# High and low parts of two weight matrices made by casting and accumulating transfers instead of by two engines

## The chip, the cores and the metric

The kernel runs on one core of one Trainium2 chip. The metric is device time in microseconds (us) for one execution of the whole layer; a profile of one execution stands beside it. The engines are named as in the profile: PE does matrix products, ACT (ScalarE) and DVE (VectorE) do elementwise work from on-chip memory and from the product banks, POOL (GpSimd) does elementwise work in on-chip memory only, and SP issues transfers. All five run their own queue in order; semaphores tie them together.

## The reference

One decoder layer over 512 tokens of width 1024, in float32, in three residual steps:

```python
y = hybrid_mixer(rms_norm(x, pre_mix_g[l]), w_in[l], attn_gn_g[l], ret_gn_g[l], w_out[l])
x = x + rms_norm(y, post_mix_g[l])
y = memory_cross_attn(rms_norm(x, pre_mem_g[l]), mem, mem_norm_g[l],
                      w_q_mem[l], w_kv_mem[l], w_o_mem[l])
x = x + rms_norm(y, post_mem_g[l])
y = swiglu(rms_norm(x, pre_ffn_g[l]), w_gate_up[l], w_down[l])
x = x + rms_norm(y, post_ffn_g[l])
```

The mixer is an input projection, eight heads of dilated window attention beside four heads of chunked retention, and an output projection. The cross attention takes its keys and values from 256 memory rows: `mh = rms_norm(mem, mem_norm_g)`, then `k, v = split(mh @ w_kv, 2)`. The feed-forward step is `(silu(h @ w_gate) * (h @ w_up)) @ w_down` with a hidden width of 2816.

## The kernel before

Products are made in the reduced format fp32r, in which PE takes 512 columns in one pass. To keep float32 accuracy every operand is held as a pair: a high part, which is the value rounded to fp32r, and a low part, which is the value minus the high part. `mm3` (L82) makes one product of two pairs from three matrix products: high by high, high by low, low by high (L84, L85, L86).

Weights come in chunks of 128 partitions x 2048 columns, 1 MB each, in a fixed list (L96): 14 of w_in, 8 of w_kv, 4 of w_out, 4 of w_q, 4 of w_o, 22 of w_gu and 11 of w_dn. `load` (L101) takes the next chunk of the list: SP issues a transfer into one of two `raw` buffers, and then `split` (L88) makes the pair in two halves of 1024 columns. For each half, ACT copies the raw values into the high part with rounding (L90), and DVE subtracts the high part from the raw values into the low part (L91). `take` (L120) hands a chunk over and calls `load` for the chunks after it, two ahead unless told otherwise. The two parts of a pair lie in two units of a pool `up` of 20 units, which the other large tiles share: transposed activations, probabilities, residual rows, the hidden values `af`. A transfer into `raw` waits only for a free raw buffer; the copy into the high part waits for a free unit.

A scheduler places the instructions of each engine in one queue from the order of the program, the free units and its own costs; what an engine finds at the head of its queue it waits for. `order` below means those queues.

Around the change the work is this. The memory keys and values (`mem_keys`, `mem_values`) are cut into twelve units of work that are put between the units of the attention heads (`filler`). Keys use w_kv chunks 0 to 3, two units `kf` to a chunk, and POOL makes the low part `kTl` of each key unit (L539). Values use chunks 4 and 5 together, then 6 and 7 together, for two blocks of rows each, and POOL makes their low part `vml` (L551). The residual rows x are loaded a second time behind the last key units. In the memory block (`mem_block`) PE makes the output projection of the cross attention for one block of 128 tokens at a time; `residual` and `normed` follow with sums of squares on ACT (L624, L153), a reciprocal square root by three Newton steps on [128, 1] tiles (`rsqrt`, L137 to L141), and the wide products on DVE (L626, L630, L635). The small steps are done on the engine that is passed as `e`: POOL in all four memory blocks and in block 3 of the mixer. The result h is transposed on PE (tp) into `h3`, the input of the gate and up projections. Those run chunk by chunk: 24 products into g and 24 into u for each of 22 chunks, then silu on ACT (L817) and a product on DVE (L820). Chunks 0 and 1 are first done for 256 tokens only, while the norms of blocks 2 and 3 are finished.

Of the kernel before, what the change touches and what calls it, by code (L numbers as in the profile page):

```python
# [11 lines left out]
F32 = mybir.dt.float32  # L12
# [4 lines left out]
ALU = mybir.AluOpType  # L17
# [21 lines left out]
def hybrid_layer(ctx, tc, t, out):  # L39
    nc = tc.nc  # L40
# [9 lines left out]
    def uname(p):  # L50
        cnt[0] += 1
        return f"{p}{cnt[0]}"
# [4 lines left out]
    def unit(name, dt=F32):  # L57
        return up.tile([P, 2048], dt, tag="u", name=uname(name))

    def pair(name):  # L60
        return unit(name + "h", F32R), unit(name + "l", F32R)
# [4 lines left out]
    def row(name):  # L66
        return wk.tile([P, D], F32, tag="w4k", name=uname(name), bufs=2)

    def junk():
        return wk.tile([P, D], BF16, tag="junk", name=uname("junk"), bufs=1)  # L70

    def small(shape, name):
        big = math.prod(shape[1:]) > 8
        return sm.tile(shape, F32, tag="big" if big else "tiny", name=uname(name), bufs=2 if big else 32)
# [13 lines left out]
    def split(src, hi, lo, scale=None):  # L88
        if scale is None:
            nc.scalar.copy(hi, src)  # L90
            nc.vector.tensor_sub(lo, src, hi.bitcast(F32))  # L91
        else:
            nc.scalar.mul(hi, src, scale)
            nc.vector.scalar_tensor_tensor(lo, src, scale, hi.bitcast(F32), op0=ALU.mult, op1=ALU.subtract)

    chunks = [(name, i) for name, idx in (  # L96
        ("w_in", range(14)), ("w_kv", range(8)), ("w_out", (2, 3, 0, 1)), ("w_q", range(4)), ("w_o", range(4)),
        ("w_gu", range(FT)), ("w_dn", range(FT // 2))) for i in idx]
    loaded = {}

    def load(pieces=1, swap=False):  # L101
        key = chunks.pop(0)
        src = t[key[0]][key[1]]
        raw = rawp.tile([P, 2048], F32, tag="raw", name=uname("raw"))
        w = pair("w")
        n = 2048 // pieces
        for i in range(pieces):
            c = slice(i * n, (i + 1) * n)
            nc.sync.dma_start(raw[:, c], src[:, c])
        n = 2048 // max(2, pieces)  # L110
        for i in range(max(2, pieces)):
            c = slice(i * n, (i + 1) * n)
            if swap and i == 0:
                nc.vector.tensor_copy(w[0][:, c], raw[:, c])
                nc.vector.tensor_sub(w[1][:, c], raw[:, c], w[0][:, c].bitcast(F32))
            else:
                split(raw[:, c], w[0][:, c], w[1][:, c])
        loaded[key] = w
# [8 lines left out]
    def ahead(name, i):  # L127
        while (name, i) in chunks:
            load()
# [20 lines left out]
    def row_rstd(rows, n, width, name, eps=EPS, e=None):  # L150
        ss = small([P, n], name + "s")
        for i, r in enumerate(rows):
            nc.scalar.activation(junk()[:, :width], r, AF.Square, accum_out=ss[:, i:i + 1])  # L153
        v = small([P, n], name + "v")
        (e or nc.vector).tensor_scalar(v, ss, 1.0 / width, eps, op0=ALU.mult, op1=ALU.add)
        return rsqrt(v, n, name, e)

    def load_rows(name):
        x = [unit("x") for _ in range(2)]
        for i in range(2):  # L160
            nc.sync.dma_start(x[i].rearrange("p (b d) -> p b d", b=2),
                              t["x"][i * 256:(i + 1) * 256, :].rearrange("(b p) d -> p b d", p=P))
        return [x[b // 2][:, (b % 2) * D:(b % 2 + 1) * D] for b in range(TB)]
# [12 lines left out]
            nc.tensor.matmul(ps[:, b * P:(b + 1) * P], lhsT=ones, rhs=dg, start=True, stop=True)  # L176
        nc.vector.tensor_copy(dst, ps[:, :n * P])

# [1 line left out]
    gT = cp.tile([P, 3, KT], F32, name="gT")  # L180
    nc.scalar.dma_start(gT, t["gT"])
    hT = [pair("hT") for _ in range(2)]
# [24 lines left out]
    x = load_rows("x")  # L207
# [41 lines left out]

    w_rqk.clear()  # L250

# [1 line left out]
    def tok_proj(c0, name, evict):  # L253
        ws = []

        def one(b):
            if b == 0:
                ws[:] = [take("w_in", c0, 1), take("w_in", c0 + 1, 2)]
            ps = bank(name)
            for k in range(KT):  # L260
                mm3(ps, hx(k, b * P, P), part(ws[k // 4], (k % 4) * 512, 512), k == 0, k == KT - 1)
            if b == TB - 1:
                ws.clear()
            evict(b, ps)

        return [lambda b=b: one(b) for b in range(TB)]
# [33 lines left out]
            nc.tensor.transpose(ps[:, b * P:(b + 1) * P], src[:, c:c + P], ident)  # L300
        split(ps, *yx(k, 0, S), gT[:, 2, k:k + 1])

# [1 line left out]
    off = [0, 512, 1024, 896]  # L304
    inn, key, state = {}, {}, {}

# [58 lines left out]
    def ret_out(h):  # L365
        y_transposed(rg, 4 + h)

# [1 line left out]
    qk = [unit("qk", F32R) for _ in range(4)]  # L369
    kl = unit("kl", F32R)  # L370
    av = unit("av")
# [46 lines left out]
    def evict_av(b, ps):  # L418
        nc.scalar.mul(av[:, b * 512:(b + 1) * 512], ps, rstd0[:, b:b + 1])

# [1 line left out]
    scale = AD ** -0.5  # L422
    poff = [512 + 384, 1024, 512, 0]
    sbank = [(2, 0), (2, 256), (1, 0), (0, 0)]
# [46 lines left out]
    def att_values(h):  # L471
        pr, hh = h // 2, h % 2
        rows = slice(hh * 64, hh * 64 + 64)
        if hh == 0:
            oTb[pr] = bank("oT")
        u = pTs.pop(h)
        for kb in range(TB):
            nc.tensor.matmul(oTb[pr][rows, kb * P:S], lhsT=av[:, kb * 512 + h * AD:kb * 512 + (h + 1) * AD],
                             rhs=u[:, off[kb]:off[kb] + S - kb * P], start=kb == 0, stop=kb == TB - 1)
        if hh == 1:  # L480
            ot = work("ot")
            nc.scalar.copy(ot, oTb.pop(pr))
            oTb[pr] = ot
# [23 lines left out]
    def att_out(pr):  # L507
        y_transposed(ya, pr)

# [1 line left out]
    mem = {}  # L511

    def mem_prepare():
# [72 lines left out]
    for i in range(AH):  # L586
# [10 lines left out]
        if i % 3 == 2:  # L597
            filler()
        att_values(i)
# [1 line left out]
    x = load_rows("x")  # L601
    g1 = load_gain("post_mix_g")
    ret_out(0)
# [12 lines left out]
    def residual(pss, b, g, e=None, cuts=((0, 512), (512, 512))):  # L616
        e = e or nc.vector
        ss = small([P, len(cuts)], "ps")
        z = row("z")
        v = small([P, 1], "pv")  # L620
        for i, (c0, n) in enumerate(cuts):
            c = slice(c0, c0 + n)
            ps = pss[c0 // 512][:, c0 % 512:c0 % 512 + n]
            nc.scalar.activation(junk()[:, :n], ps, AF.Square, accum_out=ss[:, i:i + 1])  # L624
            e.tensor_scalar(v, ss[:, i:i + 1], 1.0 / D, v if i else EPS, op0=ALU.mult, op1=ALU.add)
            nc.vector.tensor_mul(z[:, c], ps, g[:, c])  # L626
        rs = rsqrt(v, 1, "pr", e)
        for c0, n in cuts:
            c = slice(c0, c0 + n)
            nc.vector.scalar_tensor_tensor(x[b][:, c], z[:, c], rs, x[b][:, c], op0=ALU.mult, op1=ALU.add)  # L630

    def normed(b, g, e=None):
        rs = row_rstd([x[b]], 1, D, "nr", e=e)
        h = row("h")
        nc.vector.scalar_tensor_tensor(h, x[b], rs, g, op0=ALU.mult, op1=ALU.mult)  # L635
        return h
# [12 lines left out]
    def out_proj(bs, lhs, ws, ks, name, outer, mid=None):  # L649
        pss = {b: [bank(name) for _ in range(2)] for b in bs}  # L650

        def one(b, n, i):
            k = ks[i]
            mm3(pss[b][n], lhs(k, b), part(ws[k // 2], (k % 2) * D + n * 512, 512), i == 0, i == KT - 1)

        for c in range(outer):
            for b in bs:
                for n in range(2):
                    for i in (2 * c, 2 * c + 1):
                        one(b, n, i)  # L660
        for b in bs:
            for n in range(2):
                if mid and (b, n) == (bs[-1], 1 if len(bs) == 1 else 0):
                    mid()
                for i in range(2 * outer, KT):
                    one(b, n, i)
        return pss
# [8 lines left out]
    def mix_half(hf, mid=None):  # L676
        bs = (2 * hf, 2 * hf + 1)
        pss = out_proj(bs, y_lhs, w_out, order, "o1", 2, mid)
        hs = []
        for b in bs:  # L680
            e = nc.gpsimd if b == 3 else nc.vector
            residual(pss[b], b, g1, e)
            hs.append(normed(b, g2, e))
        return hs
# [83 lines left out]
    wo = [take("w_o", c, 0) for c in range(4)]  # L768
    g3 = load_gain("post_mem_g")
# [6 lines left out]
    nat = tuple(range(KT))  # L776
    g4 = load_gain("pre_ffn_g")
    h3 = [pair("h3") for _ in range(2)]

    def mem_block(b, mid=None):  # L780
        residual(out_proj((b,), o_lhs, wo, nat, "o2", 0, mid)[b], b, g3, nc.gpsimd)
        return normed(b, g4, nc.gpsimd)

    def h3_block(h, b):
        transposed(h, lambda half: [a.rearrange("p (k s) -> p k s", k=4) for a in h3[half]], S, b * P)
# [15 lines left out]
    to_h3(ha, 1)  # L801
    hc = mem_block(3)

# [1 line left out]
    af = []  # L805

    def gx(k, c0, n):
# [15 lines left out]
    for f in range(2):  # L823
        w, pg, pu = take("w_gu", f), bank("g"), bank("u")
# [9 lines left out]
    for f in range(2, FT):  # L834
        w, pg, pu = take("w_gu", f), bank("g"), bank("u")
# [23 lines left out]
    for c in range(FT // 2 - NL):  # L859
        if c % 2 == 0:  # L860
            split_a(c // 2)
        w = take("w_dn", c)
# [111 lines left out]
```

## Time and profile before

| what | value |
|---|---|
| device time, median of 2 runs | 830.46 us (830.09 to 830.82) |
| span of the profiled execution, first to last instruction | 828.5 us |
| median less span | 1.96 us |
| PE busy | 807.9 us (98%) |
| DVE busy | 396.6 us (48%) |
| ACT busy | 305.4 us (37%) |
| POOL busy | 132.8 us (16%) |
| transfers | 85.86 MB, 104 GB/s over the span |
| mean granted TensorE clock | 0.991 |

The page gives no separate device time for the profiled execution. Its span is set beside the median of the runs, and the difference of 1.96 us is carried along as what lies around the span. A row that groups instructions gives their sum, their mean in ns and the idle time of the engine ahead of them. A product's row lasts longer than its slot, since products overlap in the array: the distance between two starts is what one costs.

### The profile page before, as it was taken

To read this page: it belongs to the slowest core of one execution; us is meant where nothing else is said; L and a number is where in the kernel's file an instruction comes from. 1 tells how busy PE (TensorE), PEld (TensorE's weight loads), DVE (VectorE), ACT (ScalarE), POOL (GpSimd) and SP (SyncE) were. 2 spreads that over 40 slices of the span, in tenths; PEclk is the share of its full clock that TensorE was granted. 3 is DMA by queue.
4 is the path that set the end of the run, shared out by engine and by line. 5 is a ranking of instruction groups with operands and counts; after the bars stand their busy time and mean duration, and the time that the engine had idled before them with its cause. 6 is when DMAs were issued, how large, how long until landed. Compare 5 with 4: busy or idle time off the path is not lost. (4 is left out here: it accounts for less than half of the span.)

```text
span 828.5 us, 10220 instructions
## 1 busy us (share of the span) xinstructions
PE 807.9 (98%) x4108; PEld 675.7 (82%) x4108; DVE 396.6 (48%) x766; ACT 305.4 (37%) x537; POOL 132.8 (16%) x176
## 2 busy tenths in 40 slices
PE   9979999999999999999999899999999999999996
PEld 7768888877777878999988788888888888888884
DVE  5595168764565657758446441405050314222144
ACT  5504333466464733445435232222130305332110
POOL 0161024410110100300036300000000004236000
PEclk9998999999999999999999999999999999999998
DMA  8726212221124440524002340505050322521011
GB/s 305 291 77 236 94 51 87 73 95 52 51 70 175 163 153 0 197 109 153 1 1 102 127 153 1 203 1 203 1 203 1 121 82 74 182 102 51 1 51 51
DMA packets 15519, 85.86 MB, mean 104 GB/s; under 512 B 1904, under 2 KB 1904, under 8 KB 6896
## 3 DMA queue, kind: packets, MB, share of 16 engines
q1 hardware_dynamic: 14752, 84.16, 27.7%
q10 hardware_dynamic: 720, 1.06, 0.3%
q8 instruction: 32, 0.52, 0.3%
q14 instruction: 15, 0.12, 0.0%
HBM read 83.11 MB, written 2.10 MB: 103 GB/s over the span
## 5 line engine op out<-in xcount | busy, mean ns | idle before, releaser
L91 DVE TENSOR_TENSOR wl<-raw,wh 128x1024 fp32r<-128x1024 f32 (+1 forms) x135 | 166.5, 1267 | 102.6 <-ACT wh L90 70.2
L90 ACT CAST wh<-raw 128x1024 fp32r<-128x1024 f32 (+1 forms) x135 | 133.8, 1042 | 95.3 <-DMA raw<-in_w_in 38.1
L820 DVE TENSOR_TENSOR af<-sg,u 128x512 f32<-128x512 f32 x22 | 15.1, 686 | 133.7 <-PE u L86 133.7
L846 POOL TENSOR_TENSOR al<-af,ah 128x512 fp32r<-128x512 f32 x22 | 34.6, 1605 | 257.5 <-ACT ah L845 243.3
L84 PE MATMUL g<-h3h,wh 128*128 128x512 f32 (+1 forms) x192 | 72.1, 375 | 0.0
L84 PE MATMUL u<-h3h,wh 128*128 128x512 f32 (+1 forms) x192 | 71.7, 373 | 0.0
L85 PE MATMUL g<-h3l,wh 128*128 128x512 f32 (+1 forms) x192 | 71.3, 371 | 0.0
L86 PE MATMUL g<-h3h,wl 128*128 128x512 f32 (+1 forms) x192 | 71.3, 371 | 0.0
L85 PE MATMUL u<-h3l,wh 128*128 128x512 f32 (+1 forms) x192 | 71.3, 371 | 0.0
L86 PE MATMUL u<-h3h,wl 128*128 128x512 f32 (+1 forms) x192 | 71.3, 371 | 0.0
L84 PE MATMUL dn<-wh,ah 128*128 128x512 f32 x176 | 68.5, 389 | 0.0
L85 PE MATMUL dn<-wl,ah 128*128 128x512 f32 x176 | 68.5, 389 | 0.0
L86 PE MATMUL dn<-wh,al 128*128 128x512 f32 x176 | 68.5, 389 | 0.0
L817 ACT ACTIVATE sg<-g 128x512 f32<-128x512 f32 x22 | 13.1, 598 | 149.2 <-PE g L86 123.0
L84 PEld LDWEIGHTS g<-h3h,wh 128*128 128x128 f32 x192 | 36.5, 190 | 6.5 <-ACT h3h L90 0.2
L84 PEld LDWEIGHTS u<-h3h,wh 128*128 128x128 f32 x192 | 36.6, 191 | 6.3
L85 PEld LDWEIGHTS g<-h3l,wh 128*128 128x128 f32 x192 | 36.2, 188 | 6.4
L86 PEld LDWEIGHTS g<-h3h,wl 128*128 128x128 f32 x192 | 36.2, 188 | 6.2
L85 PEld LDWEIGHTS u<-h3l,wh 128*128 128x128 f32 x192 | 36.2, 188 | 6.2
L86 PEld LDWEIGHTS u<-h3h,wl 128*128 128x128 f32 x192 | 36.1, 188 | 6.1
L84 PEld LDWEIGHTS dn<-wh,ah 128*128 128x128 f32 x176 | 33.0, 188 | 6.9
L86 PEld LDWEIGHTS dn<-wh,al 128*128 128x128 f32 x176 | 33.0, 188 | 6.9
(267 smaller groups left out, 1752.8 us busy)
## 6 DMA issues: line engine op xcount, KB each, us to landing
raw<-in_w_gu SPq DMA_DIRECT2D x22, 1024.0 KB, 4.8
raw<-in_w_in SPq DMA_DIRECT2D x12, 1024.0 KB, 5.1
raw<-in_w_dn SPq DMA_DIRECT2D x11, 1024.0 KB, 4.7
raw<-in_w_kv SPq DMA_DIRECT2D x8, 1024.0 KB, 4.7
x<-in_x SPq DMA_DIRECT2D x4, 1024.0 KB, 10.2
raw<-in_w_out SPq DMA_DIRECT2D x4, 1024.0 KB, 5.3
raw<-in_w_q SPq DMA_DIRECT2D x4, 1024.0 KB, 5.3
raw<-in_w_o SPq DMA_DIRECT2D x4, 1024.0 KB, 4.7
```

The lines of the kernel that those rows point to most:

```text
L84: nc.tensor.matmul(o, lhsT=sh, rhs=mh, start=start, stop=False)
L85: nc.tensor.matmul(o, lhsT=sh, rhs=ml, start=False, stop=False)
L86: nc.tensor.matmul(o, lhsT=sl, rhs=mh, start=False, stop=stop)
L90: nc.scalar.copy(hi, src)
L91: nc.vector.tensor_sub(lo, src, hi.bitcast(F32))
L817: nc.scalar.activation(sg, pg, AF.Silu)
L820: nc.vector.tensor_mul(af[-1][:, (f % 4) * S:(f % 4 + 1) * S], sg, pu)
L846: nc.gpsimd.tensor_sub(lo[:, c], af[i][:, c], hi[:, c].bitcast(F32))
```

## The change

In `load`, chunks of w_kv and w_gu go another way. POOL issues a transfer from the weight straight into the high part, with a cast to fp32r on the way. ACT then writes the negated high part over 2048 columns into the low part. POOL issues a second transfer of the same 1 MB that adds the weight onto it, so that the low part becomes weight minus high part. The other weights are loaded as before. Separately, the small steps of `residual` and `normed` that ran on POOL (four memory blocks, and block 3 of the mixer) go to DVE.

```diff
     def load(pieces=1, swap=False):
         key = chunks.pop(0)
         src = t[key[0]][key[1]]
+        if key[0] in ("w_kv", "w_gu"):
+            w = pair("w")
+            nc.gpsimd.dma_start(w[0], src)
+            nc.scalar.mul(w[1], w[0].bitcast(F32), -1.0)
+            nc.gpsimd.dma_start(w[1], src, accum_op=ALU.add)
+            loaded[key] = w
+            return
         raw = rawp.tile([P, 2048], F32, tag="raw", name=uname("raw"))
...
-            e = nc.gpsimd if b == 3 else nc.vector
+            e = nc.vector
             residual(pss[b], b, g1, e)
             hs.append(normed(b, g2, e))
...
-        residual(out_proj((b,), o_lhs, wo, nat, "o2", 0, mid)[b], b, g3, nc.gpsimd)
-        return normed(b, g4, nc.gpsimd)
+        residual(out_proj((b,), o_lhs, wo, nat, "o2", 0, mid)[b], b, g3, nc.vector)
+        return normed(b, g4, nc.vector)
```

The added lines move the later lines of the file by 7. Below, H(k) is the casting transfer of chunk k of w_kv, N(k) the negation on ACT, and L(k) the accumulating transfer.

POOL's queue before, from the third-last key unit to the end of the memory values (kTl is the low part of the keys, vml that of the values):

```order
L539 TENSOR_TENSOR kTl_1524<-kf_2014,kTh_1523 128x256
L539 TENSOR_TENSOR kTl_1524<-kf_2074,kTh_1523 128x256
L539 TENSOR_TENSOR kTl_1524<-kf_2126,kTh_1523 128x256
L551 TENSOR_TENSOR vml_1526<-vf_2220,vmh_1525 128x512
L551 TENSOR_TENSOR vml_1526<-vf_2304,vmh_1525 128x512
L551 TENSOR_TENSOR vml_1526<-vf_2386,vmh_1525 128x512
L551 TENSOR_TENSOR vml_1526<-vf_2415,vmh_1525 128x512
```

POOL's queue now, at the same place (wh_2029 and wl_2030 are chunk 4, 2164 and 2165 chunk 5, 2169 and 2170 chunk 6, 2324 and 2325 chunk 7):

```order
L546 TENSOR_TENSOR kTl_1518<-kf_2002,kTh_1517 128x256
L546 TENSOR_TENSOR kTl_1518<-kf_2059,kTh_1517 128x256
L108 DMA wl_2030<-in_w_kv 128x2048
L546 TENSOR_TENSOR kTl_1518<-kf_2111,kTh_1517 128x256
L106 DMA wh_2164<-in_w_kv 128x2048
L106 DMA wh_2169<-in_w_kv 128x2048
L108 DMA wl_2165<-in_w_kv 128x2048
L108 DMA wl_2170<-in_w_kv 128x2048
L558 TENSOR_TENSOR vml_1520<-vf_2199,vmh_1519 128x512
L558 TENSOR_TENSOR vml_1520<-vf_2283,vmh_1519 128x512
L106 DMA wh_2324<-in_w_kv 128x2048
L108 DMA wl_2325<-in_w_kv 128x2048
```

H(5) now stands behind the low part of the last key unit, and H(7) behind the low part of the second value block.

ACT's queue before, from the first to the last sum of squares of memory block 3 (raw_4188 and raw_4260 are gate/up chunks):

```order
L624 ACTIVATE junk_4133,ps_4130<-o_4080 128x512
L90 CAST wh_4189<-raw_4188 128x1024 x2
L90 CAST wh_4261<-raw_4260 128x1024 x2
L624 ACTIVATE junk_4137,ps_4130<-o_4081 128x512
L153 ACTIVATE junk_4155,nrs_4154<-x_2231 128x1024
```

ACT's queue now, at the same place (wl_4159 is gate/up chunk 2, wl_4228 chunk 3):

```order
L631 ACTIVATE junk_4109,ps_4106<-o_4056 128x512
L631 ACTIVATE junk_4113,ps_4106<-o_4057 128x512
L107 ACTIVATE wl_4159<-wh_4158 128x2048
L160 ACTIVATE junk_4131,nrs_4130<-x_2210 128x1024
L107 ACTIVATE wl_4228<-wh_4227 128x2048
```

The two sums of squares of the projection now follow each other, and one negation, which waits for the casting transfer of gate/up chunk 2, stands ahead of the sum of squares of the new x.

## Prediction

> **What bounds the kernel now.** First the page: the span and the shares of the engines. Then the waits of PE, since PE is busy nearly all the time.
>
> ```profile
> span 828.5 us, 10220 instructions
> PE 807.9 (98%) x4108; PEld 675.7 (82%) x4108; DVE 396.6 (48%) x766; ACT 305.4 (37%) x537; POOL 132.8 (16%) x176
> ...
> PE rv L85 <- DVE wl L91: 5.2, 1, 5.2
> PE tp L792 <- DVE h L635: 4.0, 1, 4.0
> PE warm L215 <- POOL ones L196: 1.0, 1, 1.0
> ```
>
> PE sets the time. In 828.5 us it waits twice for more than a microsecond once it has begun its work: 5.2 us for a low part of w_in, which the change doesn't touch, and 4.0 us for h of the last memory block. No wait is on a chunk of w_kv or w_gu. So whatever is taken off DVE and ACT there can win little, and the questions are whether the 4.0 us go, and whether the new way of loading is in time everywhere.
>
> The price list comes from the groups, from the windows (columns: window, length, busy time of PE, PEld, DVE, ACT and POOL, granted clock, share of the transfer engines, GB/s) and from the issues (median us to landing last).
>
> ```profile
> L91 DVE TENSOR_TENSOR wl<-raw,wh 128x1024 fp32r<-128x1024 f32 (+1 forms) x135 | 166.5, 1267 | 102.6 <-ACT wh L90 70.2
> L90 ACT CAST wh<-raw 128x1024 fp32r<-128x1024 f32 (+1 forms) x135 | 133.8, 1042 | 95.3 <-DMA raw<-in_w_in 38.1
> ...
> 268.00:272.00 4.00, 4.00 (x21) 3.31 (x20) 2.15 (x10) 0.22 (x1) 0.00 (x0) 1.00 1.02 421
> 490.00:710.00 220.00, 220.00 (x972) 182.22 (x971) 61.13 (x60) 54.44 (x67) 13.04 (x8) 1.00 0.27 96
> ...
> raw<-in_w_kv SPq DMA_DIRECT2D x8, 1024.0 KB, 4.7
> ...
> x<-in_x SPq DMA_DIRECT2D x2, 1024.0 KB, 8.6
> ```
>
> A product of 512 columns takes a slot of 220.00 / 972 = 0.226 us. With all engines busy 421 GB/s flow, so 1 MB costs 2.5 us of the transfer engines; a 1 MB load lands after 4.7 us, so 2.2 us lie around it. Two x loads issued together, 2 MB, land after 8.6 us.
>
> **What is removed, and where it lay.** Thirty chunks no longer use ACT's two copies and DVE's two subtractions: 60 x 1.267 = 76 us of DVE work go. ACT's 60 x 1.042 = 63 us come back as 30 negations over 2048 columns, 2.1 us each at two halves' price. PE waited for none of it, so the gain is nothing, and if the estimate of the negation is off, ACT's idle 63% covers it.
>
> **The small norm steps go to DVE.** Two late products of memory block 3, the chain behind it on POOL, and the same steps on DVE at the end of the kernel (start, length, engine, line):
>
> ```profile
> 447.96 0.39 PE L85 MATMUL o<-wl,oTxh 128*128 128x512 f32 x1
> ...
> 452.27 0.39 PE L86 MATMUL o<-wh,oTxl 128*128 128x512 f32 x1
> ...
> 454.73 2.26 POOL L625 TENSOR_SCALAR pv<-ps,pv 128x1 f32<-128x1 f32 x1 [0.61 <-ACT junk L624]
> ...
> 461.44 0.27 POOL L141 TENSOR_SCALAR pry<-prw,pry 128x1 f32<-128x1 f32 x1
> 464.51 0.19 POOL L155 TENSOR_SCALAR nrv<-nrs 128x1 f32<-128x1 f32 x1 [2.81 <-ACT junk L153]
> ...
> 467.42 0.26 POOL L141 TENSOR_SCALAR nry<-nrw,nry 128x1 f32<-128x1 f32 x1
> ...
> 821.48 0.21 DVE L625 TENSOR_SCALAR pv<-ps,pv 128x1 f32<-128x1 f32 x1 [4.69 <-ACT junk L624]
> 821.61 0.68 DVE L626 TENSOR_TENSOR z<-dn,g 128x512 f32<-128x512 f32 x1
> ...
> 824.13 1.42 DVE L630 SCALAR_TENSOR_TENSOR x<-z,pry,x 128x512 f32<-128x512 f32 x2
> ```
>
> The first half took 461.71 - 454.73 = 7.0 us on POOL and takes 824.13 - 821.48 = 2.65 on DVE; the second 467.68 - 464.51 = 3.2 against 2.65 - 0.68 = 2.0. That is 5.5 us earlier, more than the 4.0 that PE waits. The negation of gate/up chunk 2 stands ahead of the sum of squares of x in ACT's queue. Its casting transfer goes out when the product at 447.96 releases its unit; by the prices below it lands at 454 and is negated by 456, before x is ready near 457.6 (last product 452.3, its sum of squares some 1.2, then 2.65 and 1.42). So it costs nothing; it would if that transfer took over 7 us.
>
> ```profile
> 458.25 1.03 PE L792 MATMUL tp<-ident,h 128*128 128x128 f32 x8
> ...
> 469.06 1.97 PE L792 MATMUL tp<-ident,h 128*128 128x128 f32 x8 [4.02 <-DVE h L635]
> ...
> 62.09 0.79 PE L85 MATMUL rv<-wl,hTh 128*128 128x512 f32 x1 [5.16 <-DVE wl L91]
> ...
> 66.09 0.48 PE L85 MATMUL rv<-wl,hTh 128*128 128x512 f32 x1
> ...
> 64.00:66.00 2.00, 2.00 (x6) 1.61 (x5) 2.00 (x3) 0.00 (x0) 0.00 (x0) 0.50 0.43 74
> ```
>
> A long wait also costs clock. After the 5.16 us one the clock is at 0.50, and nine slots take 66.09 - 62.09 = 4.0 us instead of 2.0: 2.0 us lost. After the 4.02 us one eight transposes take 1.97 instead of 1.03; I count 1.2 us. **Gain: 4.0 + 1.2 = 5.2 us.**
>
> **The memory values, first wait.** Before, chunks of w_kv were fetched into raw buffers ahead of their unit. Now the high part's transfer needs the unit, the negation needs the transfer, the second transfer needs the negation, and POOL issues both between its own work, in order. H(5) stands behind the low part of key unit 7, so it goes out late.
>
> ```profile
> 253.78 0.72 POOL L539 TENSOR_TENSOR kTl<-kf,kTh 128x256 fp32r<-128x256 f32 x1 [5.64 <-ACT kTh L538]
> ...
> 252.00 0.28 PE L86 MATMUL mk<-memTh,wl 128*128 128x256 f32 x1
> 252.12 0.60 PE L490 MATMUL otr<-ident,ot 128*128 128x128 f32 x4
> ...
> 252.65 2.37 PE L478 MATMUL oT<-pT,av 128*64 128x512 f32 x8
> ...
> 256.01 0.48 PE L84 MATMUL mv<-wh,memTh 128*128 128x512 f32 x1
> ...
> 271.35 0.39 PE L86 MATMUL mv<-wh,memTl 128*128 128x512 f32 x1
> 271.58 1.03 PE L300 MATMUL yt<-ident,rg 128*128 128x128 f32 x8
> 272.45 1.47 PE L300 MATMUL yt<-ident,ya 128*128 128x128 f32 x12
> 273.68 0.47 PE L84 MATMUL mv<-wh,memTh 128*128 128x512 f32 x1
> ...
> 274.21 1.29 POOL L551 TENSOR_TENSOR vml<-vf,vmh 128x512 fp32r<-128x512 f32 x1 [7.21 <-ACT vmh L550]
> ```
>
> H(5) can be issued from 253.78 + 0.72 = 254.5 us. The two x loads now take the units of chunk 3, free at about 252.1 when the last key product is done, and L(4) goes out at that time too. An accumulating transfer must read its target as well as its source. No row shows one; its bounds are 2.5 us of the engines (any 1 MB) and 10 us (twice the 2 MB pair), and I take 5.0, since the pair of x loads, 8.6 us to landing, is the nearest row to 2 MB moved. A cast has no row either; I take 2.5. For POOL's issue I take 1 us, between 0.2 and 2.3, the ends of its small rows in the memory block. So the engines have 5.0 + 5.0 + 2.5 = 12.5 us of work from 252.1; H(5) lands at 264.6 + 1.1 = 265.7, N(5) ends at 267.8, L(5) lands 1 + 5.0 + 2.2 = 8.2 later, at 276.0. PE, which in the new order does 13 products, one head's oT and four transposes (20 take 273.68 - 271.58 = 2.1, so 0.42) before it needs L(5), is there at 256.0 + 2.9 + 2.4 + 0.4 = 261.7. **Wait: 14.3 us; 8.6 with every transfer at 2.5, 25 with 10 and the slow issue.**
>
> What the Trainium skill says of the price: in Collectives: The Full Stack, section "The bandwidth ceiling: the fold count and why AG ≠ RS ≠ AR", an add in the transfer engines is itself free but reads two sources, so it halves the rate (ratio 1.93). By that rule this wait is the 14.3, by a plain copy's price 8.6; no run here shows it yet.
>
> **Second wait.** H(7) stands behind the low part of value block 1: from that block's last product, 271.35, to the end of the row at 274.21 + 1.29 = 275.5, are 4.15 us. Then H(7) 1 + 4.7, N(7) 2.1, L(7) 8.2: 20.2 us in all. PE meanwhile has 2.3 (to 273.68) + 24 products 5.4 + 4 transposes 0.4 + 2 products 0.5 + 18 output products 4.1 = 12.7. **Wait: 7.5 us; 3.6 to 14.** N(7) also stands ahead of ACT's copies of the first w_out chunk, but PE needs those before it needs L(7), so they only divide the wait. Both waits are long enough to cost the clock: 2 x 2.0 = 4 us.
>
> **Gate and up.** A chunk is 48 x 0.226 = 10.9 us of PE, and H and L cost 2.5 + 5.0 = 7.5 us of the transfer engines, with the units free four to five chunks ahead and the negation some 2.5 chunks (27 us) ahead of need. Hidden, at no cost; if a pair costs more than 10.9, every chunk pays the excess.
>
> **The sum.** 14.3 + 7.5 + 4 - 5.2 = +20.6 us on the span of 828.5: 849.1, and with the 1.96 around it 851 us, 2.5% above the median of 830.46.
>
> **Rivals.** A measurement of this kernel can tell about 2%, 16.6 us (813.9 to 847.1).
> - The transfers are as cheap as plain ones. Then the waits are 8.6 + 3.6, and 12.2 + 4 - 5.2 = +11 gives 841; if SP's x loads move out of the way or the chain is issued sooner, down to 825 with only the gain left. For it: 421 GB/s leave room. This is the side on which the kernel isn't slower. It decides as soon as L costs less than about 4 us of the engines.
> - The transfers bound gate and up. At 10 us for L a pair costs 12.5, an excess of 1.6 over some 20 chunks: 33 us, and waits of 25 + 14: 33 + 39 + 4 - 5.2 = +71, 901. Against it: the share of 0.27 at 96 GB/s.
> - POOL is held up when it issues. The row at 454.73 shows a small POOL step stretched to 2.26 us beside DVE's subtractions; two more us on each of H(5), L(5), H(7), L(7) give 8, 859. The Trainium skill, SBUF — State Buffer, section "Who interferes with whom", has DVE copies and tensor_scalar work lock POOL out of writing descriptors. DVE's work in those places is mostly from the product banks, which speaks against it.
> - That the cast doesn't round and the low parts come out empty would change the output, not the time.
>
> **Chances.** Forecast 0.45 (844 to 862, seven parts in eight of it above 847), cheap transfers 0.33, bound gate and up 0.15, slow issue 0.05, more gain than I see 0.02. Slower by over 2%: 0.39 + 0.15 + 0.05 = 0.59; within: 0.33 + 0.06 = 0.39; faster: 0.02. Eight in ten lie between 836 and 885: below are the cheapest cases, above most of the third.
>
> **What would show it.** In the waits of PE: mv on wl of w_kv by 14 and 7.5 us, tp on h gone, g and u with none; the casting transfer at about 5 us to landing, the accumulating one at 8. Wrong if PE never waits for w_kv, or if waits appear in every gate/up chunk.

## The result, and the profile after

The changed kernel takes 853.69 us (median of 2 runs, 852.84 to 854.55), the kernel before 830.46: a ratio of 1.028, with a 95% interval of 1.025 to 1.031. The profiled execution has a span of 851.1 us at a mean granted clock of 0.982, against 828.5 at 0.991. The forecast of 851 was short by 2.7 us.

The page of the kernel after, its span and the shares of the engines:

```profile
span 851.1 us, 10200 instructions
PE 812.5 (95%) x4108; PEld 678.2 (80%) x4108; DVE 348.8 (41%) x801; ACT 303.4 (36%) x507; POOL 138.1 (16%) x141
```

DVE is relieved of 48 us, and PE's share falls from 98% to 95%: the time went where PE stands still. The waits of PE in the kernel after (total us, times, longest):

```profile
PE mv L85 <- DMA wl<-in_w_kv: 17.6, 3, 8.9
PE rv L85 <- DVE wl L91: 5.2, 1, 5.2
PE o L84 <- ACT wh L90: 2.1, 1, 2.1
PE otr L497 <- ACT ot L489: 1.3, 1, 1.3
...
PE mv L84 <- DMA wh<-in_w_kv: 0.3, 1, 0.3
```

The wait of tp on h is gone, g and u wait for no transfer, and the memory values (mv) wait for the low parts of w_kv. The same place in order of time, PE, ACT and POOL of the kernel after together (start, length, engine, line; idle time and its releaser in brackets):

```profile
253.31 0.87 POOL L108 DMA_DIRECT2D wl<-in_w_kv  x1 [1.78 <-ACT wl L107]
255.56 1.15 POOL L106 DMA_DIRECT2D wh<-in_w_kv  x2
...
266.08 0.80 PE L85 MATMUL mv<-wl,memTh 128*128 128x512 f32 x1 [5.47 <-DMA wl<-in_w_kv]
...
269.99 1.91 ACT L107 ACTIVATE wl<-wh 128x2048 fp32r<-128x2048 f32 x1 [12.22 <-DMA wh<-in_w_kv]
...
272.19 0.87 POOL L108 DMA_DIRECT2D wl<-in_w_kv  x1 [15.48 <-ACT wl L107]
...
280.14 0.79 PE L85 MATMUL mv<-wl,memTh 128*128 128x512 f32 x1 [8.91 <-DMA wl<-in_w_kv]
...
292.37 0.39 PE L86 MATMUL mv<-wh,memTl 128*128 128x512 f32 x1
...
301.12 0.73 PE L84 MATMUL mv<-wh,memTh 128*128 128x512 f32 x2 [0.26 <-DMA wh<-in_w_kv]
304.00 1.83 PE L84 MATMUL o<-wh,yTh 128*128 128x512 f32 x5 [2.15 <-ACT wh L90]
313.24 0.50 PE L85 MATMUL mv<-wl,memTh 128*128 128x512 f32 x1 [3.24 <-DMA wl<-in_w_kv]
```

POOL issues L(4), the last low part of the keys, then H(5) and H(6) together. L(4) is 12.8 us on its way and PE waits 5.47 us for it. H(5) is 14.4 us on its way; N(5) follows, L(5) lands at 280.1, and PE waits again, 8.91 us. So the first wait is 5.47 + 8.91 = 14.4 us in two pieces, and the second 0.26 + 2.15 + 3.24 = 5.65 us in three.

What the transfer engines and the clock did meanwhile, and the gate and up stage (columns as in the windows of before; the last three are granted clock, share of the transfer engines, GB/s):

```profile
256.00:260.00 4.00, 4.00 (x22) 2.31 (x21) 2.91 (x13) 0.96 (x2) 0.72 (x2) 1.00 1.04 300
260.00:264.00 4.00, 0.61 (x4) 0.28 (x2) 0.00 (x0) 0.00 (x0) 0.00 (x0) 0.98 1.01 244
264.00:268.00 4.00, 1.92 (x5) 1.54 (x6) 0.00 (x0) 0.00 (x0) 0.00 (x0) 0.50 1.00 381
268.00:272.00 4.00, 3.23 (x9) 2.23 (x7) 0.00 (x0) 1.91 (x1) 0.00 (x0) 0.66 0.79 310
...
276.00:280.00 4.00, 0.00 (x0) 0.00 (x0) 0.00 (x0) 0.00 (x0) 0.00 (x0) 0.50 0.99 205
280.00:284.00 4.00, 3.86 (x9) 3.08 (x10) 0.00 (x0) 0.00 (x0) 0.00 (x0) 0.50 1.06 219
...
300.00:325.00 25.00, 19.35 (x78) 14.95 (x77) 11.67 (x9) 12.46 (x14) 4.52 (x3) 0.93 0.55 170
...
490.00:710.00 220.00, 219.76 (x1029) 184.32 (x1028) 18.63 (x27) 51.56 (x46) 25.34 (x36) 1.00 0.74 185
```

From 256 to 268 the engines are full. From 276 to 280 only accumulating transfers are under way: full engines move 205 GB/s there, against 421 before with plain ones. In the gate and up stage the share rises from 0.27 to 0.74, and PE stays busy. How the first 14.4 us came about is read from the DMA queues (packets, MB, share of the engines) between 252.0 and 268.2 us:

```profile
q0 software_dynamic: 261, 2.01, 46.4%
q1 hardware_dynamic: 523, 2.08, 38.9%
```

q1 is SP's queue, and its 2.08 MB are the two loads of x. q0 is POOL's; its 2.01 MB are L(4) and nearly all of H(5). 2.01 MB are less than these two, so H(6), issued together with H(5), has hardly moved, and it lands near 272.2, where ACT's negation of it starts, 2.2 us behind H(5). By the same queues no packet starts between 252.0 and 254.4, and until 258.0 only x moves, although POOL issued L(4) at 253.3.

The issues (median us to landing last) and the queue of POOL's transfers (packets, MB, share of the engines over the span):

```profile
wh<-in_w_gu POOLq DMA_DIRECT2D x22, 1024.0 KB, 10.1
wl<-in_w_gu POOLq DMA_DIRECT2D x22, 1024.0 KB, 8.3
wh<-in_w_kv POOLq DMA_DIRECT2D x8, 1024.0 KB, 6.7
wl<-in_w_kv POOLq DMA_DIRECT2D x8, 1024.0 KB, 8.6
...
q0 software_dynamic: 8640, 62.92, 29.7%
```

### The profile page after: what moved, and what is told of

Same layout as the page of the kernel before. It is cut to its first block, busy times and chain, and to the rows that moved or that the text cites. A ratio compares the mean times of both kernels' runs of the same rounds, so it can differ in the third digit from the quotient of the medians.

```text
span 851.1 us, 10200 instructions
## 1 busy us (share of the span) xinstructions
PE 812.5 (95%) x4108; PEld 678.2 (80%) x4108; DVE 348.8 (41%) x801; ACT 303.4 (36%) x507; POOL 138.1 (16%) x141
## 4 chain that ended last, share of the span: by engine, by line
PE 87%; DMA 5%; DVE 4%; issue 2%; ACT 1%; POOL 0%; SPq 0%; DVEq 0%; POOLq 0%; ACTq 0%
PE g L84 5%; PE u L86 5%; PE g L86 5%; PE g L85 5%; PE u L85 5%; PE u L84 5%; PE dn L85 5%; PE dn L84 5%; PE dn L86 5%; PE o L86 3%; PE o L85 3%; PE o L84 3%; DMA wh<-in_w_kv 2%; DMA wl<-in_w_kv 2%; PE q L84 2%; PE q L85 2%
## 5 line engine op out<-in xcount | busy, mean ns | idle before, releaser
L91 DVE TENSOR_TENSOR wl<-raw,wh 128x1024 fp32r<-128x1024 f32 (+1 forms) x75 | 97.0, 1318 | 92.5 <-ACT wh L90 63.5
L90 ACT CAST wh<-raw 128x1024 fp32r<-128x1024 f32 (+1 forms) x75 | 74.3, 1032 | 74.7 <-DMA raw<-in_w_in 36.0
L827 DVE TENSOR_TENSOR af<-sg,u 128x512 f32<-128x512 f32 x22 | 15.1, 687 | 191.4 <-PE u L86 191.4
L824 ACT ACTIVATE sg<-g 128x512 f32<-128x512 f32 x22 | 13.1, 597 | 158.5 <-PE g L86 158.5
L107 ACT ACTIVATE wl<-wh 128x2048 fp32r<-128x2048 f32 x30 | 57.2, 1912 | 28.9 <-DMA wh<-in_w_kv 20.0
L108 POOL DMA_DIRECT2D wl<-in_w_gu x22 | 19.2, 873 | 171.5 <-ACT wl L107 161.7
L106 POOL DMA_DIRECT2D wh<-in_w_gu x22 | 15.1, 735 | 163.4 <-DVE x L637 123.9
## 6 DMA issues: line engine op xcount, KB each, us to landing
wh<-in_w_gu POOLq DMA_DIRECT2D x22, 1024.0 KB, 10.1
```

What stands on the lines that cost most here:

```text
L106: nc.gpsimd.dma_start(w[0], src)
L107: nc.scalar.mul(w[1], w[0].bitcast(F32), -1.0)
L108: nc.gpsimd.dma_start(w[1], src, accum_op=ALU.add)
L824: nc.scalar.activation(sg, pg, AF.Silu)
L827: nc.vector.tensor_mul(af[-1][:, (f % 4) * S:(f % 4 + 1) * S], sg, pu)
```

## The experiments

Theory A was the prediction's: the loss is two waits ahead of the memory values and their clock; gate and up are hidden; the norm steps give some 5 us back. All edits are to the kernel after, and times are medians beside runs of the kernel before on the same chip (830.4, 829.7 and 830.5 us in the three groups of runs).

### Which matrix costs: gate/up alone, w_kv alone, w_kv's keys with gate/up

```diff
-        if key[0] in ("w_kv", "w_gu"):
+        if key[0] == "w_gu":                                        # gate/up alone
+        if key[0] == "w_kv":                                        # w_kv alone
+        if key[0] == "w_gu" or key[0] == "w_kv" and key[1] < 4:     # keys and gate/up
```

Gate/up alone:

> Only the gate/up chunks go by casting and accumulating transfers; w_kv is loaded through the raw buffers as before, and the small norm steps stay on DVE. Theory A (all of the loss lies in the memory values, and gate/up is hidden): PE waits for no wl or wh of w_kv, the 5.2 us of the norm move are kept, and the time is 830.5 - 5 = 825 us (823 to 828). Theory B (the transfers of gate/up cost something too, by sharing the transfer engines or by ACT and POOL queues): 832 us or more, with waits on g or u.

w_kv alone:

> Only the w_kv chunks go by casting and accumulating transfers; gate/up as before, norms on DVE. Theory A: the same waits on mv as in the changed kernel (5.5, 8.9, 3.2 us and smaller ones), 852 to 856 us. Theory B: less than 850 us, since the part that gate/up costs is gone.

Keys and gate/up, with the memory values' chunks 4 to 7 loaded the old way:

> Chunks 0 to 3 of w_kv (memory keys) and all gate/up chunks come by transfers, chunks 4 to 7 (memory values) by the old load and split. Theory A (the loss of w_kv lies in the two waits ahead of the memory values; the keys have 7.5 us or more of PE's work a chunk and cost nothing): 825 us (823.5 to 827), like gate/up alone with 824.6, and no wait of mv on a transfer. Rival B (the keys' loads also delay what stands behind them in ACT's or POOL's queue, or the clock): 830 us or more with a wait of mk or of the attention's o or otr.

Gate/up alone took 824.64 us (ratio 0.9930, 0.9919 to 0.9942), keys with gate/up 825.21 (0.9949, 0.9930 to 0.9968), w_kv alone 858.93 (1.0344, 1.0331 to 1.0357). The waits of PE with keys and gate/up:

```profile
PE rv L85 <- DVE wl L91: 5.1, 1, 5.1
PE warm L222 <- POOL ones L203: 1.0, 1, 1.0
PE mk L84 <- DVE amx L455: 1.0, 1, 1.0
```

No transfer is in the list. So neither the 22 chunks of gate and up nor the four chunks of the keys cost anything that can be told apart here; four chunks of 1 MB make the whole loss, 853.69 - 825.21 = 28.5 us (these two are from different groups of runs, in which the kernel before differs by 0.8 us). Gate/up alone is faster than before by 0.7%, which is under 2%, with an interval clear of 1. It has the lowest time of all that were run, but the runs do not tell it apart from keys with gate/up. w_kv alone missed its 852 to 856 by 2.9 us. Its list of waits says why:

```profile
PE mv L85 <- DMA wl<-in_w_kv: 18.0, 3, 8.7
...
PE tp L799 <- DVE h L642: 2.8, 1, 2.8
```

The wait of tp on h is there in part, although the norm steps are on DVE. That was not in Theory A.

### The norm steps: alone, and left on POOL

```diff
-        if key[0] in ("w_kv", "w_gu"):
+        if key[0] in ():                # norm steps alone: all weights loaded the old way
```

```diff
-            e = nc.vector               # loads alone: norm steps back on POOL
+            e = nc.gpsimd if b == 3 else nc.vector
...
-        residual(out_proj((b,), o_lhs, wo, nat, "o2", 0, mid)[b], b, g3, nc.vector)
-        return normed(b, g4, nc.vector)
+        residual(out_proj((b,), o_lhs, wo, nat, "o2", 0, mid)[b], b, g3, nc.gpsimd)
+        return normed(b, g4, nc.gpsimd)
```

> No chunk goes the new way; only the small norm steps have moved from POOL to DVE. Theory A: the 4.0 us wait of tp on h and its slow clock go, 825 us (823 to 827). Rival: the small steps are now held up behind DVE's subtractions for gate/up chunks, which are still there, and the gain is under 2 us, 828.5 or more.

> Both weights go the new way, the small norm steps stay on POOL. Theory A: as the changed kernel plus the 5.2 us that the move gained, 857 to 861 us. Rival: POOL's steps now stand behind transfers that wait for a unit or for ACT, so that the memory blocks are held up as well: 865 us or more, with waits of tp on h over 6 us.

The norm steps alone gave 827.20 us (0.9966, 0.9955 to 0.9977), between the two expectations: 3.2 us, not 5.2. DVE's queue in that kernel shows what stands in the way:

```profile
453.35 3.49 DVE L91 TENSOR_TENSOR wl<-raw,wh 128x1024 fp32r<-128x1024 f32 x3
456.75 0.21 DVE L632 TENSOR_SCALAR pv<-ps,pv 128x1 f32<-128x1 f32 x1
```

and in the kernel with gate/up by transfers alone, at the same place:

```profile
453.37 0.21 DVE L632 TENSOR_SCALAR pv<-ps,pv 128x1 f32<-128x1 f32 x1 [1.51 <-ACT junk L631]
```

Three low parts of gate/up chunks, 3.49 us, stand ahead of the small steps once those are in DVE's queue. With the subtractions gone too, the remaining 2.8 us of waiting go: 827.20 - 824.64 = 2.6 us. The gain needs both halves of the change.

The loads without the norm steps gave 866.13 us (1.0434, 1.0421 to 1.0447), as the rival had it, 12.4 us more than the change as a whole. POOL's queue in that kernel, and PE's wait:

```profile
481.00 0.92 POOL L108 DMA_DIRECT2D wl<-in_w_gu  x1 [4.12 <-ACT wl L107]
481.65 0.59 POOL L148 TENSOR_SCALAR pry<-prw,pry 128x1 f32<-128x1 f32 x1
...
494.56 0.93 POOL L108 DMA_DIRECT2D wl<-in_w_gu  x1 [3.27 <-ACT wl L107]
...
505.27 1.97 PE L799 MATMUL tp<-ident,h 128*128 128x128 f32 x8 [8.53 <-DVE h L642]
```

The Newton steps stand in POOL's queue behind accumulating transfers that wait for a negation. Putting them on DVE is what makes transfers from POOL bearable in this stage.

### What the first wait is made of: the addition, the loads of x, and the chain

```diff
-            nc.gpsimd.dma_start(w[1], src, accum_op=ALU.add)
+            nc.gpsimd.dma_start(w[1], src)          # no addition
```

```diff
-    x = load_rows("x")                              # x later
-    g1 = load_gain("post_mix_g")
     ret_out(0)
...
     filler(9)
+    x = load_rows("x")
+    g1 = load_gain("post_mix_g")
     att_out(3)
```

No addition:

> Leaves out the addition: the second transfer of a pair copies instead of accumulating, so the low parts are not low parts; the same transfers of the same sizes in the same order otherwise. Theory A (an accumulating MB holds the 16 engines twice as long as a copied one, 5.1 us against about 2.6, and that is a part of the waits of the memory values): two accumulating transfers lie in front of the first wait (chunks 4 and 5) and one in the second, so the first falls from 14.4 us to about 9 and the second from 5.6 to about 3, and the clock gives 1 to 2 us back: 844 us (840 to 848), and the landing of the second transfer of gate/up falls from 8.3 to about 6 us. Rival B (the length of the chain of two landings and a negation makes the waits, not the engine time of the addition): the waits stay within 2 us of 14.4 and 5.6, 851 to 855 us.

x later:

> The four loads of x and the gain's load are issued after the last memory values instead of ahead of the retention's output, so they no longer share the engines with the transfers of chunks 4 and 5. Theory A (shared engines: 4 MB of x, about 10 us of engine time, lie ahead of the landing of the accumulating transfer of chunk 4 and the casting transfer of chunk 5): the first piece of the first wait (5.5 us) falls to about 1, the second (8.9) to 7 to 9, since chunk 5's chain of cast, negation and accumulation still takes about 15 us from its issue at 255.6; first wait 8 to 10 instead of 14.4, 847 us (844 to 850) unless x, now loaded around 314 beside w_out, comes too late for the residual sums, which would show as a wait of z or h. Rival B (the order of the POOL queue and the chain's own length make the whole wait, x's loads only fill idle engines): 14.4 stays within 2 us, 852 to 855.

Both edits together:

> Leaves out the addition and issues the loads of x after the last memory values. It leaves of the first wait what the chain alone costs: from the casting transfer of chunk 5, issued near 255.4, about 6 us to landing, 1.9 for the negation, 0.5 and 5.2 for the second transfer, so it lands near 269.5. Theory A (first wait of 14.4 us = x's loads on the shared engines + the double price of accumulating + a chain that is longer than PE's work ahead of it): PE is there near 263.3, so about 6 us are left, no wait for chunk 4, and about 841 us (838 to 844). Rival B (the two parts hide each other, each removed alone uncovers the other): 9 us or more are left, as without the addition alone, 843 to 846.

Without the addition the kernel takes 843.75 us (1.0158, 1.0139 to 1.0176), with x later 851.67 (1.0261, 1.0245 to 1.0276), with both 840.75 (1.0125, 1.0094 to 1.0156). PE's waits for the first pair of value chunks, without the addition:

```profile
264.72 0.50 PE L85 MATMUL mv<-wl,memTh 128*128 128x512 f32 x1 [1.44 <-DMA wl<-in_w_kv]
268.46 0.50 PE L84 MATMUL mv<-wh,memTh 128*128 128x512 f32 x1 [0.94 <-DMA wh<-in_w_kv]
275.64 0.79 PE L85 MATMUL mv<-wl,memTh 128*128 128x512 f32 x1 [6.68 <-DMA wl<-in_w_kv]
```

with x later:

```profile
261.70 0.50 PE L85 MATMUL mv<-wl,memTh 128*128 128x512 f32 x1 [1.24 <-DMA wl<-in_w_kv]
274.13 0.79 PE L85 MATMUL mv<-wl,memTh 128*128 128x512 f32 x1 [9.40 <-DMA wl<-in_w_kv]
```

and with both, ACT, POOL and PE together:

```profile
255.62 1.11 POOL L106 DMA_DIRECT2D wh<-in_w_kv  x2
...
262.24 1.92 ACT L107 ACTIVATE wl<-wh 128x2048 fp32r<-128x2048 f32 x1 [4.42 <-DMA wh<-in_w_kv]
...
264.45 0.53 POOL L108 DMA_DIRECT2D wl<-in_w_kv  x1 [7.72 <-ACT wl L107]
...
269.55 0.80 PE L85 MATMUL mv<-wl,memTh 128*128 128x512 f32 x1 [5.94 <-DMA wl<-in_w_kv]
```

The first wait is 14.4 us in the change, 9.1 without the addition, 10.6 with x later, 5.9 with both. The two parts, 5.3 and 3.7 us, nearly add up (8.4 of 9.0), and 5.9 us are the bare chain: H(5) goes out at 255.6, and PE needs L(5) 8.0 us later, while a cast, a negation and a second transfer take 14. The rivals fall in all three by the first wait. By the time, x later is a miss: 851.67 lies outside the 844 to 850 expected, and only 2.0 us of the 3.7 come out at the end. The loads of x then lie beside H(7), the second wait grows from 5.65 to 6.8 us, and the single wait of 9.4 us is followed by a longer stretch at half clock. That expectation also speaks of 4 MB of x; the profile shows two loads of 1 MB.

The price of the addition is also in the queue's share. Without the addition, the page has:

```profile
q0 software_dynamic: 8640, 62.92, 21.0%
```

Sixty casts take 0.210 x 842.8 = 177 us of the engines, 2.95 us each. With the addition it is 0.297 x 851.1 = 253 us; less thirty casts at 2.95, an accumulating transfer takes 5.5 us, a ratio of 1.86. The rule of the Trainium skill that the prediction used (Collectives: The Full Stack, section "The bandwidth ceiling: the fold count and why AG ≠ RS ≠ AR": an add reads two sources, ratio 1.93) agrees with that in size; the runs show the price and not the reason for it.

### Whether gate and up are hidden because a pair fits

```diff
             nc.gpsimd.dma_start(w[1], src, accum_op=ALU.add)
+            if key[0] == "w_gu":
+                nc.gpsimd.dma_start(w[1], src, accum_op=ALU.add)
```

> Gate/up alone gets its accumulating transfer twice (the weight is added a second time, so the values are others). Theory A (gate/up is hidden because the engine work of a pair, about 8 us by shares of 0.74 to 0.80 of 10.9 us, fits into the 10.9 us that PE works on a chunk): with 5.1 us more, 13.2 to 13.8 us a chunk, the loads become the bound; 2.3 to 2.9 us over PE's time for some 18 of the 22 chunks is 41 to 52 us, with up to 10 us for a lower clock behind the waits: 895 to 915 us, waits of g and u on accumulating transfers in the list of PE's waits, and an engine share near 1 in the gate/up stage. Rival B (the accumulation is limited by something other than engine time, such as latency, and more of them overlap): under 870 us, share below 0.95.

It took 940.49 us (1.1332, 1.1313 to 1.1351), more than either theory. The waits, and the stage in one window:

```profile
PE g L86 <- DMA wl<-in_w_gu: 63.2, 15, 8.0
```

```profile
490.00:790.00 300.00, 243.94 (x1078) 200.36 (x1077) 20.49 (x30) 54.30 (x47) 44.62 (x58) 0.92 0.91 215
```

The loads are the bound, as Theory A said: with 2.95 + 5.5 + 5.5 = 13.9 us the three transfers of a chunk are 3.0 us over PE's 10.9, which is 66 us over all 22 chunks, and the list has 63.2. The rest of the miss is the clock, whose mean is 0.954 against 0.982: PE is busy for 836.3 us instead of 812.5 with the same products, 23.8 us more, where 10 were allowed. 63 + 24 = 87 answers the 86.8 us over the change.

### POOL's order

```diff
-        nc.gpsimd.tensor_sub(lo, kf[:, :NM], hi.bitcast(F32))
+        nc.vector.tensor_sub(lo, kf[:, :NM], hi.bitcast(F32))
...
-        nc.gpsimd.tensor_sub(lo, vf, hi.bitcast(F32))
+        nc.vector.tensor_sub(lo, vf, hi.bitcast(F32))
```

> The low parts of keys and values (kTl, vml) are subtracted by DVE instead of POOL, so that nothing but transfers stands ahead of the casting transfers of chunks 5 and 7 in POOL's queue. Rival (POOL's order makes the waits: the transfers stand behind the low parts): the casting transfer of chunk 5 goes out up to 2.5 us earlier (253.3 instead of 255.6) and that of chunk 7 up to 2 us earlier, and both waits shorten by as much: 849 to 851 us. Theory A (chunk 5's transfer stands behind the accumulating transfer of chunk 4 and x's loads on the engines anyway, so its landing does not move): at most the second wait shortens, by 1 to 2 us: 852 to 853 us.

It took 854.45 us (1.0285, 1.0263 to 1.0306), no different from the change. POOL and ACT in it:

```profile
252.98 1.42 POOL L106 DMA_DIRECT2D wh<-in_w_kv  x2
...
268.17 1.91 ACT L107 ACTIVATE wl<-wh 128x2048 fp32r<-128x2048 f32 x1 [11.01 <-DMA wh<-in_w_kv]
```

H(5) goes out 2.6 us earlier and lands 1.8 us earlier, after 15.2 us on its way instead of 14.4. The first wait is 13.1 instead of 14.4 us, but the output product then waits 3.0 for its weight instead of 2.1, and the end does not move. The rival of 849 to 851 us falls, and for the first wait POOL's order isn't the cause: what H(5) meets on the engines is. For the second wait this run settles nothing: H(7) goes out 7.2 us earlier (288.8 instead of 296.0), but its negation only 0.9 us earlier (300.2 instead of 301.1), since in this kernel it stands in ACT's queue behind a copy of yTh that waits for PE.

## Why the prediction was right, point by point

**The sum.** Predicted +20.6 us on the span; it is +22.6. Keys with gate/up, the kernel without the values' chunks, splits it: 28.5 us of loss where 14.3 + 7.5 + 4 = 25.8 were put, and about 5 us of gain where 5.2 were put. The loss by its rows: waits of 14.4 + 5.65, another 1.3 of otr on ACT that belongs to the same place, and for the clock 6.3 us: after the waits 12, 11 and 18 products take 5.0, 4.6 and 6.0 us instead of 2.7, 2.5 and 4.1. That is 27.6 in all. The other 0.9 us have no row of their own.

**First wait, 14.3 predicted, 14.4 measured: right in size by luck, wrong in its working.** The step that failed is "12.5 us of work from 252.1; H(5) lands at 264.6 + 1.1 = 265.7". It landed at 270.0, 4.3 us later. Some 2.3 us of that is the start: L(4) and x were issued at 253.3 and 253.4, and the first packet moved at 254.4. Another 1.3 is the work: by the two rows of the DMA queues it was (0.464 + 0.389) x 16.2 = 13.8 us. POOL's two transfers took the 7.5 that were put; x took 6.3 where 5.0 were put. The last 0.7 is the end: H(5) landed 1.8 us after 268.2, where 1.1 were put. H(6) has no part in this sum, since it lands behind H(5). The size came out because PE was late too. The prediction had L(4) in time, while it took 12.8 us among the loads of x and cost 5.47, and the products after it ran at clocks of 0.50 and 0.66, so PE came to L(5) at 271.2 instead of 261.7, with 8.91 us of waiting left.

**Prices.** L was taken at 5.0 us of the engines and costs 5.5, the cast at 2.5 and 2.95, the negation at 2.1 and 1.91. All close. The bounds of 2.5 to 10 for L were the widest thing in the sum, and the rival of cheap transfers hung on them: 841 us if L costs as much as a cast. The kernel without the addition, where it does, took 843.75. So that rival's account was right but for its condition; the price of the addition decided between the two. Its waits of 8.6 and 3.6 do not follow from the prediction's own figures: with 1 us for each issue and 2.5 for L they are 9.3 and 5.0, which gives 843.6 us. The upper waits, 25 and 14, come out as 25.6 and 15.1.

**Second wait, 7.5 predicted, 5.65 measured.** The chain was put at 20.2 us from the last product of value block 1 to the landing of L(7); by the rows at 292.37 and 313.24 it took 20.9. What was off is PE's work beside it: 20.9 - 5.65 = 15.2 us, where 12.7 were counted, and 1.9 of the difference is the clock: the 18 output products took 6.0 us instead of 4.1. N(7) stands ahead of ACT's copies of the first w_out chunk and divides the wait, as said: a wait of 2.1 us or more on that chunk stays in every kernel here that loads chunk 7 this way, even without the addition.

**Clock, 4 predicted, 6.3 by the rows.** Two slow stretches of 2.0 us were counted, and there were three, of 2.3, 2.1 and 1.9 us.

**Norm steps, 5.2 predicted; gate/up alone gains 5.8 us.** The size is right, its cause was half right. "PE waited for none of it, so the gain is nothing" was said of DVE's subtractions. It was true of the kernel before, where the small steps were on POOL, and false once they share DVE's queue: alone the move gains 3.2 us, and the other 2.6 come from the subtractions that leave. And what the prediction didn't price at all is what the move saves inside the change, 12.4 us, since the steps would have stood behind waiting transfers on POOL.

**Negation of gate/up chunk 2 ahead of the sum of squares.** It costs nothing, as said:

```profile
470.07 1.94 ACT L107 ACTIVATE wl<-wh 128x2048 fp32r<-128x2048 f32 x1
474.36 1.06 ACT L160 ACTIVATE junk<-x 128x1024 bf16<-128x1024 f32 x1 [2.34 <-DVE x L637]
```

The negation ends 2.3 us before x is ready.

**Gate and up, hidden.** A pair costs 8.4 us of the engines (0.74 of 10.9 is 8.1), not 7.5, and is hidden. With 13.9 us a chunk the loads set the time; where between the two it turns, no run shows. The rival of the bound stage was right in its mechanism and wrong in L's price.

**What would show it.** The landing of the accumulating transfer was put at 8 us and is 8.3 to 8.6. That of the casting transfer was put at 5 and is 6.7 for w_kv and 10.1 for gate/up. Without the addition it is 5.7 and 7.1: the same transfers land later when they are queued with accumulating ones, so a landing time alone does not tell what a transfer costs.

**POOL held up when it issues.** It wasn't. The issues of L(4) and L(5) take 0.87 us each, those of H(5) and H(6) together 1.15, where 1 us each was taken and 3 feared.

What stays open: w_kv alone is 5.2 us slower than the whole change, of which its wait of 2.8 us and its clock (0.979 against 0.982, 2.6 us) are the parts that rows show, and no run took those two apart. The second wait is less well separated than the first: without the addition 0.21 + 2.15 us of it are left, and nothing else in its chain was varied alone.

## What to carry to other kernels

Count the engine time of every transfer that is issued within the same stretch, not only those on the chain, and count it from the issue: two loads of x held the engines for 6.3 of the 13.8 us up to H(5), and moving them away shortened the first wait by 3.7 us. A chain of load, work and second load is hidden where a stage runs long and even (22 chunks here cost nothing with a pair at 8.4 of 10.9 us), and is bare at the first chunk whose place in memory comes free late: convert the loads of a stage only from where its lead is longer than the chain. When two steps trade engines in one change, price each also without the other, since the queue that one step joins may be the one that the other empties.

## What the runs showed that was not expected

A second transfer that accumulates occupied the engines for 5.5 us a MB against 2.95 for a cast, and full engines moved 205 GB/s in it. A second addition on every gate/up chunk cost more in clock than was allowed for: 63 us of waits in 15 places brought the mean granted clock from 0.982 to 0.954, and PE was busy 23.8 us longer with the same products. An accumulating transfer that POOL issued at 253.3 did not move until 258.0, while a load of x that SP had issued 0.1 us later was moving. Moving a transfer's issue 2.6 us ahead, with the engines full, moved its landing by 1.8 us and the end not at all.
